# A layer kernel bound by TensorE: another table for the order of instructions on each engine

## The chip, the cores and the metric

One core of a Trainium2 chip runs the whole program. Its engines are TensorE (PE, with its weight loads PEld), VectorE (DVE), ScalarE (ACT), GpSimd (POOL) and SyncE (SP, which here only issues transfers). Times are microseconds on the device, the median over the executions shown. The trace comes from one further, profiled execution.

## The reference

One decoder layer on x of 512 tokens by 1024 channels, in float32. Two mixers read one input projection: native sparse attention with 8 heads of 64 (compressed blocks, the 8 best blocks, and a window, weighed by gates), and gated DeltaNet with 4 heads of 128. DeltaNet, cut to its core:

```python
qkv = jax.nn.silu(causal_dwconv(qkv, conv_w))        # a filter of 4 taps
T = lax.linalg.triangular_solve(eye + m, ...)        # inside each chunk
u, w = T @ (v * beta[..., None]), T @ (kb * jnp.exp(gcum)[..., None])
def step(state, xs):                                 # from chunk to chunk
    v_new = un - wn @ state
    o = (qn * jnp.exp(gn)[..., None]) @ state + an @ v_new
    state = state * jnp.exp(g_last)[..., None] + kn'.T @ v_new
```

The two results are merged with gates and projected, and x <- LN(alpha*x + mix). Then a gated MLP of width 2816 with a causal filter of width 3 follows, and a second LN.

## The kernel before

**Products.** A float32 product is made of fp32r matmuls. A weight block arrives as `raw` (SP's transfer, 128x1024), and `split_w` (L458) makes two halves of it: `wh` is the rounded part (L468 on ACT, L470 elsewhere) and `wl` what is left (L472). `product` (L477) then issues three matmuls for each k: L482 with wh, L484 with the activations' low part, L485 with wl. Small products and transposes run as fp32 with 128 columns or fewer: L657 transposes the DeltaNet tiles, L1073 the attention scores.

**Stages.** Up to about 320 us the program works through attention heads (`scores` and `attn`: L1040 and L1041 make scores, L1044 to L1057 the softmax, L1076 and L1077 the split of the transposed scores, L1087 and L1093 the sums over values) and DeltaNet heads (`gdn_mid`, `gdn_tri`, `gdn_inv`, `gdn_out`), mixed with each other and with the input projection. Then come the rest of the projection, the merge (L1119, L1197, L1199), the output projection and a LN, the FFN's up-projections with filter and gate (L1405 to L1414, some 480 to 700 us), and the down-projection with the last LN.

**The state recurrence.** `gdn_out` (L829) walks four chunks of a head. Each chunk is a chain: PE L838 multiplies by the state, DVE L840 makes r, PE L844 multiplies by z, ACT L846 copies it as vn, PE L854 makes the step, DVE L857 the new state, then the next chunk. L849 and L862 make the output beside it. `conv_silu` (L633) filters a head's input: ACT scales a tap (L640), POOL adds it (L641), ACT makes a tanh (L646), POOL multiplies (L650). In `gdn_inv`, L771 to L792 solve the triangular system; DVE's L788 makes ym, which PE's L791 multiplies.

**Transfers.** SP issues the loads of weights into three `raw` buffers, and the stores of the result (L1497). POOL issues sums of weight blocks in DRAM (L501 for the output projection's osum, L511 for the down-projection's wsum), some of which add to what an earlier one wrote and so wait for it.

**What sets the order.** Each engine runs its instructions strictly in its own order. `QUEUES` (from L133) is a table of numbers: for each engine the positions, in the order in which the code issues them, that are to run one after another. `queues` (L335) walks it and ties each instruction to the one ahead of it, for scheduling alone. Whatever else an instruction waits for (data, buffers) stays as it is.

Of the kernel before, what the change touches and what calls it, by code (L numbers as in the profile page):

```python
# [144 lines left out]
746 761 560-561 762-764 552 765-768 562 565-566 553 769 554 537-538 563 539 564 540 567 591-592 581-582 568-569 555  # L145
570 593-596 556 597 557 598 558 770-771 599-600 583 559 585-586 772 796-798 773 571-572 584 573 587 574-577 774
601-602 799-801 578 802 579 803 603 588 580 804 606 805 589 604 590 607 806-807 651 808-809 652 810 608 605 811-812
620-621 609-611 653 813-815 654 612 622-626 613-618 627-630 641-642 864-872 643-644 619 631 873 645-646 874 632-634
647-648 635 699 649-650 700 875 636-638 876 639-640 877-879 701 816 880 704 881 702-703 705 882-887 706 718-719
707-709 817-819 720 710 838-839 721-722 655-657 659 658 660-662 840 854 711 855 663-666 841 712-713 842 714 843 715  # L150
667-669 671-678 670 856 716 858 717 844-845 860 857 679-686 861 846 859 862 687-694 863 847-848 1053 695-698 747-750
936-938 1054 939-943 775-778 944-945 1055-1056 779 1057 946-948 780 949-951 781-782 1058-1059 849 952-954 783-784 977
955 978 785 956 979-981 786-787 1060 850 957 851 958 788-789 959 1072 790 982-983 1073 791-792 984-988 793 989-990
794-795 991-992 852 993-1008 853 1009 1074-1075 1061 1076 1062 820-821 824-825 1010-1012 822-823 826 1101 827-829 1029
1063 1102 830 832-833 831 1103-1108 1030 1013-1014 1031-1040 834 1015 835 1041-1045 836-837 1046-1050 888-890 1051
1064 1052 1065 891 1016-1018 1077-1100 1066 1019-1021 1067 1109-1111 1022 1068 1023-1024 1069-1070 892 896-897 893-895
898-899 1112 1203 1071 1205-1208 900-903 1209 1113 1204 1114-1115 1219 1116 1220 1117 1210 904 908-915 905-907
1211-1212 1221 1213 1223 1214 1118-1120 1224 916-923 1215-1217 1222 924-931 1121-1122 1218 932-935 1225-1226 1233-1234
1123 960 1227-1228 1124-1125 961 1126-1127 962-963 1128-1131 964-965 1132-1133 966 1141-1142 967-968 1134-1136
1143-1144 1235 969-970 1145-1147 971 1148-1150 1238 1151-1153 1236 972-973 1239 1179-1180 1237 974 1240 975 1241 1181  # L160
1252-1253 1154-1155 1182 1242 976 1243 1156 1183 1157-1158 1184-1185 1159 1186 1160-1162 1254 1187 1257 1163 1244-1245
1164 1188 1255-1256 1025 1137-1140 1259 1258 1246 1026 1189-1198 1283 1247 1199-1200 1273 1201 1274 1284 1202 1285
1027-1028 1165 1260 1166-1167 1248 1286 1261-1262 1307 1169-1170 1308-1311 1168 1171-1172 1275 1173 1249 1312 1250
1174 1251 1277-1278 1263 1287 1313-1315 1276 1175-1177 1279 1178 1316-1317 1403-1404 1318 1264 1319-1320 1405
1288-1289 1406 1280 1265-1267 1408 1268 1407 1281-1282 1269 1409 1270 1321-1323 1271 1324 1229 1325 1290 1272
1326-1327 1291 1328-1329 1230 1330 1410 1292 1422 1293 1423 1294 1231-1232 1424 1411-1413 1425-1426 1295-1298 1414
1299-1301 1427 1302-1304 1379 1428 1415 1380-1381 1416 1429-1432 1417-1419 1305 1382 1443 1420 1444 1331-1332 1421
1383 1306 1384-1385 1445 1386 1447-1448 1433 1387 1434 1388 1435 1389-1392 1436-1437 1333 1449 1446 1393 1453 1477
1454 1478 1394 1438 1450 1455-1456 1451 1439 1395 1458 1452 1440 1396-1397 1479 1459 1480 1441 1481 1442 1482 1334
1460-1462 1457 1463 1472-1473 1398 1483-1485 1399-1401 1486 1402 1487-1488 1474 1464 1501-1502 1465-1466 1475-1476  # L170
1467 1582 1489 1583 1490 1335 1503 1468 1517-1518 1339-1341 1504 1342 1336-1338 1505-1506 1491-1494 1343-1346
1519-1520 1469 1495 1521 1470 1347-1348 1522 1351-1358 1349 1471 1507-1508 1350 1509-1511 1496-1499 1512-1513
1359-1366 1523-1524 1544 1500 1545 1584-1585 1546 1367-1374 1525 1514 1547-1550 1610-1611 1515-1516 1586-1588
1375-1378 1551 1526 1612-1613 1527 1552-1554 1589 1614 1528 1615 1563-1564 1529-1530 1590 1616 1591-1592 1531-1532
1617-1618 1533 1555 1619 1593 1534 1594 1535 1556 1595 1620 1596 1536-1537 1597-1598 1538 1565 1599 1621-1622
1539-1540 1566-1567 1557-1558 1568-1569 1559 1600-1602 1541-1542 1570 1560 1571 1561 1623-1626 1543 1562 1603 1627
1604-1605 1572-1577 1628-1629 1634 1630 1635 1631 1636-1639 1632 1640-1641 1578 1606-1609 1579 1642-1643 1658 1644
1633 1645-1646 1580-1581 1647 1659-1660 1648 1661-1662 1649 1663-1667 1650-1651 1668-1670 1652-1654 1671 1682 1655
1672 1656-1657 1673-1675 1683-1685 1676-1680 1686-1687 1681 1694 1688-1692 1695 1693 1706-1707 1696 1708-1709 1718
1697-1698 1710-1711 1699-1700 1712-1714 1701 1715-1716 1702 1719 1703-1705 1720 1717 1721-1723 1730 1724-1728 1742  # L180
# [1389 lines left out]
```

## Time and profile before

| | us |
|---|---|
| median of 3 executions (lowest, highest) | 823.32 (821.67, 828.16) |
| the profiled execution | 826.54 |
| its span, first to last instruction | 824.8 |
| PE busy | 805.9 |
| DVE busy | 601.6 |
| ACT busy | 409.7 |
| POOL busy | 181.6 |

The mean granted clock of TensorE is 0.994 of full speed. An engine's busy time counts its instructions from start to end; a matmul that starts before the one ahead of it has ended doesn't count twice. In a timeline a row's time covers the instructions that are merged into it (x2, x3), and the brackets tell how long the engine stood idle ahead of it and what ended that.

### The profile page before, as it was taken

Reading aid. Unit: us, or ns where it says so; the run is one execution under the profiler, and the core shown is the slowest. Engines: PE = TensorE matmul, PEld = TensorE weight load, DVE = VectorE, ACT = ScalarE, POOL = GpSimd, SP = SyncE. Lnnn points to the kernel's source line nnn. Section 1 sums busy time; section 2 is a strip of 40 time slices with the busy share of each in tenths; the row PEclk is TensorE's granted clock in tenths of the full one; section 3 lists DMA queues with packets and bytes.
Section 4 is the critical chain, followed back from the end, with each engine's and each line's share of the span. In section 5 each row is a group of like instructions: output and inputs, shape, how many; then the busy total and the mean of one; then the engine's idle time right before and its main releaser. Section 6 shows DMA issues by size and latency. Waiting matters only on the chain.

```text
span 824.8 us, 11773 instructions
## 1 busy us (share of the span) xinstructions
PE 805.9 (98%) x4138; PEld 671.2 (81%) x4138; DVE 601.6 (73%) x1339; ACT 409.7 (50%) x912; POOL 181.6 (22%) x176
## 2 busy tenths in 40 slices
PE   9999999999899999999999999999999999999996
PEld 8788888787788888888787898888888888787774
DVE  5667689989858965565668955667566677687888
ACT  4453577774477764522344234344444444574641
POOL 0344834032283111052200111111111110100001
PEclk9999999999999999999999999999999999999998
DMA  8327180013577014344247482685238932475583
GB/s 280 106 79 281 63 268 27 26 52 125 111 183 182 27 52 103 128 140 135 83 182 250 130 165 86 235 182 163 89 112 240 222 103 90 140 212 171 185 257 132
DMA packets 43979, 119.58 MB, mean 145 GB/s; under 512 B 3472, under 2 KB 4624, under 8 KB 43664
## 3 DMA queue, kind: packets, MB, share of 16 engines
q1 hardware_dynamic: 32144, 87.37, 32.8%
q0 software_dynamic: 11776, 31.46, 16.6%
q8 instruction: 33, 0.54, 0.3%
q14 instruction: 26, 0.21, 0.1%
HBM read 116.72 MB, written 33.55 MB: 182 GB/s over the span
## 4 chain that ended last, share of the span: by engine, by line
PE 86%; DVE 6%; DMA 3%; ACT 2%; issue 1%; SPq 1%; POOL 0%; DVEq 0%; ACTq 0%
PE pu L484 10%; PE pu L482 10%; PE pu L485 10%; PE gps L482 9%; PE gps L484 9%; PE gps L485 8%; PE px L1450 5%; PE pz L1450 3%; PE pout L1087 2%; PE aps L1073 2%; PE pm L484 2%; PE pm L482 2%; PE pm L485 2%; PE pu L1450 2%; PE dps L657 1%; PE pw L1286 1%
## 5 line engine op out<-in xcount | busy, mean ns | idle before, releaser
L472 DVE TENSOR_TENSOR wl<-raw,wh 128x512 fp32r<-128x512 f32 x146 | 105.8, 728 | 74.0 <-PE pu L485 33.4
L468 ACT ACTIVATE wh<-raw 128x512 fp32r<-128x512 f32 x126 | 79.1, 629 | 140.7 <-PE pu L484 91.5
L485 PE MATMUL pu<-mh,wl 128*128 128x512 f32 (+1 forms) x384 | 130.9, 373 | 0.0
L484 PE MATMUL pu<-ml,wh 128*128 128x512 f32 (+1 forms) x384 | 130.9, 373 | 0.0
L482 PE MATMUL pu<-mh,wh 128*128 128x512 f32 (+1 forms) x384 | 130.4, 373 | 0.0
L482 PE MATMUL gps<-xh,wh 128*128 128x512 f32 x320 | 125.3, 402 | 2.4 <-ACT mt L1119 1.5
L484 PE MATMUL gps<-xl,wh 128*128 128x512 f32 x320 | 125.1, 400 | 0.0
L485 PE MATMUL gps<-xh,wl 128*128 128x512 f32 x320 | 123.2, 399 | 0.0
L485 PEld LDWEIGHTS pu<-mh,wl 128*128 128x128 f32 x384 | 71.5, 188 | 12.8
L482 PEld LDWEIGHTS pu<-mh,wh 128*128 128x128 f32 x384 | 71.3, 188 | 12.7
L484 PEld LDWEIGHTS pu<-ml,wh 128*128 128x128 f32 x384 | 71.2, 188 | 12.7 <-DVE ml L1266 0.2
L1414 POOL TENSOR_TENSOR fth<-fth,fa 128x512 f32<-128x512 f32 x22 | 31.3, 1429 | 211.7 <-DVE fth L1413 179.8
L1408 DVE SCALAR_TENSOR_TENSOR fa<-pu,fcw,fa 128x511 f32<-128x511 f32 (+1 forms) x88 | 64.5, 745 | 15.9 <-ACT fa L1405 15.4
L482 PEld LDWEIGHTS gps<-xh,wh 128*128 128x128 f32 x320 | 60.3, 189 | 13.9 <-issue 2.9
L485 PEld LDWEIGHTS gps<-xh,wl 128*128 128x128 f32 x320 | 60.2, 189 | 11.0 <-POOL wl L472 0.3
L484 PEld LDWEIGHTS gps<-xl,wh 128*128 128x128 f32 x320 | 60.4, 189 | 10.5
L1385 ACT ACTIVATE wh<-raw 128x512 fp32r<-128x512 f32 x67 | 40.2, 626 | 41.5 <-DMA raw<-wsum 12.0
L1386 DVE TENSOR_TENSOR wl<-raw,wh 128x512 fp32r<-128x512 f32 x67 | 44.8, 694 | 19.1 <-ACT wh L1385 18.5
L472 POOL TENSOR_TENSOR wl<-raw,wh 128x512 fp32r<-128x512 f32 x30 | 40.3, 1346 | 13.6 <-ACT wh L468 7.9
L523 POOL TENSOR_TENSOR rs<-rs,minus_half 128x1 f32<-128x1 f32 x8 | 7.3, 910 | 160.3 <-DVE rs L1244 108.2
L1046 ACT ACTIVATE sc<-sc,mn 128x384 f32<-128x384 f32 (+2 forms) x64 | 35.6, 558 | 9.9 <-DVE mn L1044 9.8
L1405 ACT ACTIVATE fa<-pu,fcw 128x512 f32<-128x512 f32 x44 | 29.6, 680 | 21.6 <-PE pu L485 18.3
(365 smaller groups left out, 1712.3 us busy)
## 6 DMA issues: line engine op xcount, KB each, us to landing
raw<-in_up SPq DMA_DIRECT2D x44, 512.0 KB, 3.8
raw<-in_wT SPq DMA_DIRECT2D x40, 512.0 KB, 3.6
wsum<-in_down POOLq DMA_DIRECT2D x6, 2816.0 KB, 21.8
raw<-wsum SPq DMA_DIRECT2D x20, 512.0 KB, 4.0
raw<-in_down SPq DMA_DIRECT2D x15, 512.0 KB, 4.1
osum<-in_wo POOLq DMA_DIRECT2D x6, 1024.0 KB, 9.9
wsum<-wsum POOLq DMA_DIRECT2D x2, 2816.0 KB, 14.2
raw<-in_wm SPq DMA_DIRECT2D x8, 512.0 KB, 3.5
```

The source lines that it names most:

```text
L468: A.activation(wh, r, AF.Copy)
L472: eng.tensor_tensor(wl, r, wh.bitcast(F32), op=OP.subtract)
L482: i = PE.matmul(ps, wh[k], mh_(k), start=(k == 0), stop=False)
L484: PE.matmul(ps, wh[k], ml_(k), start=False, stop=False)
L485: PE.matmul(ps, wl[k], mh_(k), start=False, stop=(k == n - 1))
L1046: A.activation(s[:, i, :n], s[:, i, :n], AF.Exp, scale=-1.0, bias=mn[:, 0, i:i + 1], accum_out=mn[:, 1, i:i + 1])
L1385: A.activation(hi, raw[:, i], AF.Copy)
L1386: V.tensor_tensor(lo, raw[:, i], hi.bitcast(F32), op=OP.subtract)
L1405: A.activation(acc, ps, AF.Copy, scale=w[:, 2:3])
L1408: V.scalar_tensor_tensor(acc[:, n:], ps[:, :S - n], w[:, i:i + 1], acc[:, n:], op0=OP.mult, op1=OP.add)
L1414: G.tensor_tensor(th, th, g[1], op=OP.mult)
L1450: m = PE.matmul(ps, a[x][:, j, ts], w[y], start=first and i == 0, stop=last and i == 2, skip_group_check=True)
```

## The change

Only the numbers in `QUEUES` differ, for all five queues, so the code below the table stands one line higher. The instructions, their operands and their buffers are the same. The order on PE is the same up to 126 us, on DVE up to 178, on ACT up to 202, on POOL up to 228 and on SP up to 799 us of the profiled execution. The table was made anew with two rules changed: a short GpSimd operation counts as handing its turn to the next one, and runs of fp32 work on TensorE are joined where that can be done. Two of its lines, as the diff shows them (the other rows are numbers of the same kind):

```diff
-37 140 62 26 41 45 54 48 55 42 36 49 51 47 52 64 66 65 67 46 68 57 69 58 50 53 56 59 61 108 104 63 109 75 60 76 80 92
+37 140 62 26 41 45 54 48 55 42 36 49 51 47 52 64 66 65 67 46 68 57 69 58 50 53 56 59 61 108 104 63 109 75 60 76 80 88
...
-173-178 168 179-180 172 182 166 170 181 183-184""",
+173-180 170 166 182 168 172 181 183-184""",
```

What that moves is seen in the engines' orders. In them gps is a product that is being summed up (2641 a projection, 2883 and 2971 two more), dps a DeltaNet product, aps and pout attention ones.

PE at about 202 us of the profiled execution, before:

```order
L482 MATMUL gps_2641<-xh_93,wh_2637 128x512
L657 MATMUL dps_2334<-ident_322,vraw_2290 128x128 x3
L484 MATMUL gps_2641<-xl_94,wh_2637 128x512
L1087 MATMUL pout_2700<-pth_345,vcat_108 128x512
L485 MATMUL gps_2641<-xh_93,wl_2639 128x512
L1087 MATMUL pout_2700<-ptl_346,vcat_108 128x512
L657 MATMUL dps_2334<-ident_322,vraw_2290 128x128
L482 MATMUL gps_2578<-xh_93,wh_2574 128x512
L484 MATMUL gps_2578<-xl_94,wh_2574 128x512
```

and now:

```order
L481 MATMUL gps_2641<-xh_93,wh_2637 128x512
L483 MATMUL gps_2641<-xl_94,wh_2637 128x512
L1086 MATMUL pout_2700<-pth_345,vcat_108 128x512
L484 MATMUL gps_2641<-xh_93,wl_2639 128x512
L1086 MATMUL pout_2700<-ptl_346,vcat_108 128x512
L656 MATMUL dps_2334<-ident_322,vraw_2290 128x128 x4
L481 MATMUL gps_2578<-xh_93,wh_2574 128x512
```

The four fp32 transposes of vraw stand together, where three and one stood before.

DVE at about 231.5 us, in the state recurrence of DeltaNet's head 2 (L857 makes the new state, L840 makes r), before:

```order
L840 SCALAR_TENSOR_TENSOR r_2473<-dps_2471,gk_1937,vb_2339 128x128
L875 SCALAR_TENSOR_TENSOR gs_2605<-gt_2603,gps_2578 128x512
L857 SCALAR_TENSOR_TENSOR state_2485<-state_2466,eg_341,dps_2483 128x128
L1048 RECIPROCAL mn_3131<-mn_3131 128x1
L1048 RECIPROCAL mn_3057<-mn_3057 128x1
L840 SCALAR_TENSOR_TENSOR r_2492<-dps_2490,gk_1937,vb_2339 128x128
L864 TENSOR_TENSOR ot_2459<-dps_2487,oi_2481 128x128
L1018 TENSOR_TENSOR pcl_2799<-aps_2793,pch_2798 128x512
```

and now:

```order
L839 SCALAR_TENSOR_TENSOR r_2473<-dps_2471,gk_1937,vb_2339 128x128
L865 COPY ot_2459<-dps_2468 128x128
L1047 RECIPROCAL mn_3057<-mn_3057 128x1
L1017 TENSOR_TENSOR pcl_2799<-aps_2793,pch_2798 128x512
L874 SCALAR_TENSOR_TENSOR gs_2605<-gt_2603,gps_2578 128x512
L1076 TENSOR_TENSOR ptl_346<-aps_3064,pth_345 128x2x2x128
L856 SCALAR_TENSOR_TENSOR state_2485<-state_2466,eg_341,dps_2483 128x128
L1098 TENSOR_TENSOR oT_2255<-pout_2700,ob_3029 64x512
L1047 RECIPROCAL mn_3131<-mn_3131 128x1
L863 TENSOR_TENSOR ot_2459<-dps_2487,oi_2481 128x128
L839 SCALAR_TENSOR_TENSOR r_2492<-dps_2490,gk_1937,vb_2339 128x128
```

Three whole-tile operations stand between the first r and the new state, where one stood, and another one ahead of the second r.

POOL at about 231.5 to 247 us, before:

```order
L501 DMA osum3_107<-osum2_106 512x512
L511 DMA wsum0_100<-in_down 1408x1x512
L1057 TENSOR_SCALAR sc_3056<-sc_3056,mn_3057,gsig_109 128x384
L472 TENSOR_TENSOR wl_2881<-raw_2873,wh_2879 128x512
L472 TENSOR_TENSOR wl_2965<-raw_2961,wh_2963 128x512
L641 TENSOR_TENSOR acc_2838<-acc_2838,tap_2842 128x509
L650 TENSOR_TENSOR th_2845<-th_2845,acc_2838 128x512
L501 DMA osum0_104<-in_wo 512x1x512
L1066 CAST vm_111<-vcb_344 32x128
```

and now:

```order
L1056 TENSOR_SCALAR sc_3056<-sc_3056,mn_3057,gsig_109 128x384
L500 DMA osum3_107<-osum2_106 512x512
L471 TENSOR_TENSOR wl_2881<-raw_2873,wh_2879 128x512
L640 TENSOR_TENSOR acc_2838<-acc_2838,tap_2842 128x509
L471 TENSOR_TENSOR wl_2965<-raw_2961,wh_2963 128x512
L649 TENSOR_TENSOR th_2845<-th_2845,acc_2838 128x512
L650 TENSOR_TENSOR kq_2802<-th_2845,acc_2838 128x4x128
```

Two issues and a CAST have gone from here to later places, and the tap-add has changed places with the weight split behind which it stood.

## Rows read from the trace of the kernel before

**Rows 1.** The page: busy time, share of the span and instructions of each engine; and the chain that ended last, by engine.

```profile
PE 805.9 (98%) x4138; PEld 671.2 (81%) x4138; DVE 601.6 (73%) x1339; ACT 409.7 (50%) x912; POOL 181.6 (22%) x176
...
PE 86%; DVE 6%; DMA 3%; ACT 2%; issue 1%; SPq 1%; POOL 0%; DVEq 0%; ACTq 0%
```

**Rows 2.** Busy time by stretch. Columns: the stretch, its length, then busy us (instructions) of PE, PEld, DVE, ACT and POOL, the granted clock, the DMA share and GB/s.

```profile
126.00:228.00 102.00, 96.57 (x610) 80.27 (x609) 91.21 (x282) 64.64 (x180) 30.65 (x33) 0.98 0.26 73
228.00:323.00 95.00, 95.00 (x580) 80.40 (x578) 71.32 (x239) 65.00 (x186) 33.36 (x35) 1.00 0.47 106
...
480.00:700.00 220.00, 220.00 (x1012) 183.58 (x1011) 144.76 (x236) 92.41 (x158) 30.89 (x22) 1.00 0.58 156
```

**Rows 3.** Who waited for whom, PE's two longest. Columns: the waiting instruction, what it waited for, us in total, times, the longest.

```profile
PE dps L791 <- DVE ym L788: 2.4, 1, 2.4
PE gps L482 <- ACT mt L1119: 1.5, 1, 1.5
```

**Rows 4.** The timeline from 211 to 218 us: POOL, then one row of DVE, then one of PE. Columns: start, us, engine, line, operation, out<-in.

```profile
212.47 1.16 POOL L470 CAST wh<-raw 128x512 fp32r<-128x512 f32 x1
213.03 1.82 POOL L741 TENSOR_TENSOR at<-at,cst 128x512 f32<-128x512 f32 x1
214.27 1.80 POOL L472 TENSOR_TENSOR wl<-raw,wh 128x512 fp32r<-128x512 f32 x1
...
212.48 4.15 DVE L472 TENSOR_TENSOR wl<-raw,wh 128x512 fp32r<-128x512 f32 x1
...
217.11 1.08 PE L791 MATMUL dps<-ym,x 128*128 128x64 f32 x8 [2.43 <-DVE ym L788]
```

**Rows 5.** Busy time of the four microseconds behind it, columns as in rows 2.

```profile
218.00:222.00 4.00, 4.00 (x13) 2.95 (x12) 2.55 (x12) 0.88 (x4) 0.00 (x0) 0.57 0.53 97
```

**Rows 6.** The timeline of PE around 202 us and, in its last two rows, at 306.77 us.

```profile
201.87 0.39 PE L482 MATMUL gps<-xh,wh 128*128 128x512 f32 x1
...
203.70 0.39 PE L484 MATMUL gps<-xl,wh 128*128 128x512 f32 x1
...
204.16 0.40 PE L482 MATMUL gps<-xh,wh 128*128 128x512 f32 x1
...
208.96 0.39 PE L482 MATMUL gps<-xh,wh 128*128 128x512 f32 x1
...
306.77 0.38 PE L844 MATMUL dps<-vb,z 128*128 128x128 f32 x2
306.99 0.49 PE L1073 MATMUL aps<-ident,sc 128*128 128x128 f32 x3
```

**Rows 7.** The timeline of DeltaNet's head 2, 231 to 243 us: PE, then DVE, then ACT.

```profile
233.18 0.38 PE L854 MATMUL dps<-vn,kd 128*128 128x128 f32 x2
...
234.08 0.41 PE L838 MATMUL dps<-state,kq 128*128 128x128 f32 x2
...
239.85 0.39 PE L844 MATMUL dps<-r,z 128*128 128x128 f32 x2
...
242.03 0.39 PE L862 MATMUL dps<-vn,at 128*128 128x128 f32 x2
...
233.60 0.35 DVE L857 SCALAR_TENSOR_TENSOR state<-state,eg,dps 128x128 f32<-128x128 f32 x1 [1.01 <-PE dps L854]
...
234.99 0.68 DVE L1018 TENSOR_TENSOR pcl<-aps,pch 128x512 fp32r<-128x512 f32 x1
...
239.88 0.63 ACT L646 ACTIVATE th<-acc 128x512 f32<-128x512 f32 x1 [0.59 <-POOL acc L641]
240.41 0.26 ACT L846 ACTIVATE vn<-dps 128x128 f32<-128x128 f32 x1
```

**Rows 8.** The timeline of POOL, 232 to 269 us.

```profile
232.41 1.75 POOL L511 DMA_DIRECT2D wsum<-in_down  x1
...
236.97 1.30 POOL L472 TENSOR_TENSOR wl<-raw,wh 128x512 fp32r<-128x512 f32 x1 [0.76 <-ACT wh L468]
238.56 1.28 POOL L641 TENSOR_TENSOR acc<-acc,tap 128x509 f32<-128x509 f32 x1 [0.29 <-ACT tap L640]
240.58 1.30 POOL L650 TENSOR_TENSOR th<-th,acc 128x512 f32<-128x512 f32 x1 [0.74 <-ACT th L646]
241.83 1.22 POOL L501 DMA_DIRECT2D osum<-in_wo  x1
...
268.16 0.61 POOL L470 CAST wh<-raw 128x512 fp32r<-128x512 f32 x1 [3.97 <-issue]
```

**Rows 9.** Transfers of weight blocks: the view of issues (KB each, median us from issue to landing) for 232 to 254 us and for 262 to 300 us, then the issue at 263.87 and the first reader of its block in the timeline.

```profile
raw<-in_wT SPq DMA_DIRECT2D x3, 512.0 KB, 7.2
...
raw<-in_wT SPq DMA_DIRECT2D x3, 512.0 KB, 3.5
...
263.87 0.33 SPq L461 DMA_DIRECT2D raw<-in_wT  x1
...
288.89 0.63 ACT L468 ACTIVATE wh<-raw 128x512 fp32r<-128x512 f32 x1
```

**Rows 10.** The FFN's beginning: POOL's first L1414 and the ACT instruction that waits for it, in the timeline, and the transfer that POOL had issued before, in the view of issues.

```profile
494.30 1.75 POOL L1414 TENSOR_TENSOR fth<-fth,fa 128x512 f32<-128x512 f32 x1 [16.94 <-DVE fth L1413]
...
509.06 0.67 ACT L1405 ACTIVATE fa<-pu,fcw 128x512 f32<-128x512 f32 x1
...
wsum<-in_down POOLq DMA_DIRECT2D x1, 2816.0 KB, 20.6
```

More of the change, by code (lines that the diff above doesn't have):

```diff
@@ new lines @@
+1308 1170 1309-1312 1275 1171-1174 1277-1278 1313-1314 1287 1315-1317 1175-1176 1276 1279-1280 1177-1178 1251 1263
+1403-1404 1264 1318-1319 1265-1266 1281 1405-1406 1282 1407 1267-1268 1408 1269 1409 1270 1288 1320-1322 1289-1290
+1323 1271-1272 1229 1324-1329 1410 1330 1230 1422 1291-1293 1423 1411-1412 1424-1425 1413 1426 1231 1294-1295
+1427-1428 1232 1296-1297 1414 1298-1300 1379 1301 1380 1302-1303 1381 1304-1305 1415-1417 1429-1432 1418 1382
+1443-1445 1331 1419 1306 1383-1384 1447 1420 1448 1421 1433 1385 1434 1386-1387 1477 1388-1389 1478 1390-1391 1435
@@ new lines @@
+1811-1812 1819-1820 1793 1821 1813 1822-1823 1826 1794 1824 1827 1825 1795 1828 1796 1829-1830 1797-1801 1831-1837
+1850-1851 1838 1852 1839 1853-1855 1840 1856-1859 1841 1860-1862 1842 1863 1843-1844 1864 1845 1874 1846 1875 1847
+1876 1865 1848 1877 1849 1866 1878-1880 1867 1881-1882 1868 1886 1883 1887-1888 1884 1889-1892 1885 1893-1894 1898
+1895-1896 1899 1869 1900 1870 1897 1901-1907 1871-1872 1908-1910 1873 1911-1915 1922 1916-1917 1923 1918 1924
+1919-1920 1925-1929 1921 1930-1932 1946-1947 1933 1948-1951 1934 1952 1935 1958-1960 1953 1936 1961-1966 1954
@@ new lines @@
+2087 2115 2098 2102 2078 2116 2079-2080 2118 2084 2105 2119 2103 2085 2123 2120 2086 2088-2089 2121 2104 2106-2107
+2124-2125 2129-2131 2122 2108-2110 2135 2141 2111-2112 2138 2136 2113 2126 2139 2127 2142-2143 2128 2147 2137
+2132-2133 2148 2140 2144 2134 2145-2146 2150 2149 2151-2153 2162 2154 2156-2157 2155 2163 2158-2161 2164 2168-2170
+2174-2176 2180-2182 2189-2190 2165-2167 2171-2173 2186-2187 2177-2179 2188 2183 2192-2194 2198 2184 2191 2185 2199
+2195 2200 2204 2196-2197 2205-2206 2201-2202 2210-2213 2203 2207-2209 2218-2220 2224-2225 2221-2222 2226 2223
@@ new lines @@
+2506 2497 2507-2508 2472 2509 2498-2499 2473 2457 2510 2474 2500 2511-2514 2501 2475 2502 2515-2517 2476 2503-2504
+2477 2518 2505 2478 2519-2521 2479-2481 2530-2533 2522 2534 2523-2524 2535-2539 2525 2540-2541 2526 2542-2543 2527
+2544-2545 2554-2555 2528-2529 2556-2557 2546 2558-2559 2547-2550 2560-2563 2551 2564-2565 2552-2553 2566-2570
+2578-2581 2571 2582-2586 2572 2587-2591 2573 2592-2593 2602-2603 2574-2575 2604 2576 2605 2577 2606 2594 2607
+2595-2596 2608-2613 2597-2599 2614-2615 2626-2627 2600 2616 2628-2632 2601 2633 2617-2619 2634-2635 2620-2621
@@ new lines @@
+2636-2637 2622 2638 2623 2639 2650 2624 2651 2640 2625 2652-2653 2641-2642 2654-2655 2643-2644 2656-2659 2645
+2660-2661 2646-2647 2662-2663 2674 2648 2664-2666 2649 2667-2670 2675-2676 2671 2677-2679 2672-2673 2680-2685 2698
+2686 2699-2702 2687 2703-2705 2688 2706-2711 2689-2690 2712 2691 2722-2723 2713 2724 2714 2692-2693 2715 2694 2716
+2725-2728 2695-2696 2717 2697 2729-2733 2718-2719 2734 2720 2735 2746 2736 2747-2749 2737-2739 2721 2750-2752 2740
+2753-2754 2741 2755-2756 2742 2757-2758 2743 2759-2763 2770-2777 2744 2778-2780 2745 2781 2764-2766 2794 2782
@@ new lines @@
+2946 2912 2947 2913 2948 2931 2949-2950 2932-2933 2962-2963 2934-2935 2951-2952 2964 2953 2936 2965-2966 2954
+2967-2970 2955 2971-2972 2937 2956-2958 2973 2959 2986 2974 2960 2975 2961 2987-2990 2976-2977 2991-2993 2978-2980
+2994-2995 2981 2996 2982 2997-2998 2983 2999-3001 2984 3002 3010 3003 2985 3004 3011 3005-3006 3012 3007 3013-3014
+3008-3009 3015-3018 3034 3019-3020 3035 3021-3022 3036 3023 3037-3044 3024 3045 3025 3046 3026 3058 3047-3048 3027
+3059-3060 3028-3029 3061 3030 3049 3031-3032 3062-3063 3050 3033 3051-3052 3064-3065 3053 3066-3068 3054-3055
@@ new lines @@
+3069-3071 3082 3056-3057 3072 3083-3092 3073-3074 3093 3075-3076 3106-3107 3077-3079 3108 3094-3097 3109-3112 3080
+3113 3098 3081 3114-3115 3099 3116-3117 3100-3103 3130 3104-3105 3118 3131-3135 3119 3136-3140 3120-3121 3141-3143
+3154 3122-3123 3155 3124 3156 3125 3144 3157 3126-3128 3158 3129 3159-3160 3145 3161-3164 3146 3165-3167 3147 3178
+3168 3148 3169-3170 3179-3181 3171 3149 3172 3182 3150-3153 3183-3185 3173 3186-3191 3174-3177 3202 3192-3199
+3203-3204 3200 3205-3210 3201 3211-3212 3226 3213-3219 3227-3232 3220-3225 3233-3236 3250 3237-3238 3251-3252
@@ new lines @@
+3239-3240 3253-3262 3241-3242 3263-3264 3274-3275 3243 3276-3277 3244 3265 3245 3278-3279 3246 3280 3247-3248 3281
+3266 3282 3249 3267 3283-3287 3268-3269 3288 3270-3271 3298 3289 3272 3290 3299-3303 3273 3304-3305 3291 3306 3292
+3307 3293-3295 3308 3296-3297 3309-3313 3322 3314 3323-3327 3315 3328 3316 3329-3334 3317 3335-3338 3318-3319
+3339-3340 3320 3346 3341 3321 3342-3344 3347 3345 3348-3353 3370 3354-3358 3371-3373 3359-3360 3374 3361-3362
+3375-3380 3363 3381 3364-3366 3394-3395 3382 3396 3383 3397 3384 3398-3399 3367-3369 3400-3402 3385 3403-3404 3386
@@ L321 @@
[L321 to L324 removed]
+302 240 232-233 273-274 234 241 275 235 305 276 242 286 303 287-288 306 243 289 252 244 304 245-246 312 311 314 313
```

285 lines of the change are left out of this document (120 added, 165 removed), and 3 rows, old and new, of the table QUEUES.

## The prediction

> **What bounds the kernel now.** I read the page's busy times and chain first: PE is busy for 805.9 us of the span, 98%, and 86% of the chain that ended last is PE [rows 1]. So a term counts only if it changes what PE waits for, or how long PE's own instructions take. Then I cut the span where the two orders part company. PE's own queue is the same up to 126 us, and between 126 and 228 us only a few instructions are exchanged. From 228 to 323 us (two DeltaNet heads mixed with attention) all five compute queues are reordered. From 480 to 700 us (the FFN's up-projections) PE's matmuls are exchanged by the hundred, but between two products that are both ready. The table of busy time by stretch shows what each has to give [rows 2]: 126 to 228 us has 102.00 - 96.57 = 5.43 us of PE idle time; 228 to 323 us has none (95.00 of 95.00); 480 to 700 us has none (220.00 of 220.00). The stretch that changes most has nothing idle to win back.
>
> The list of who waited for whom names the idle time: 2.4 us for DVE's ym (L788) and 1.5 us for ACT's mt (L1119) are the two longest [rows 3]. The timeline shows how the first one comes about [rows 4]: DVE's weight split L472 begins at 212.48, beside a Pool CAST that begins at 212.47, and takes 4.15 us, until Pool's L470, L741 and L472 have all gone by; ym stands behind it on DVE, and PE's L791 begins at 217.11 after 2.43 us of idleness. From 218 to 222 us the granted clock is 0.57 [rows 5], between full speed (2.4 GHz) and half (1.2 GHz): a loss of 0.43 x 4.00 = 1.7 us. This place is worth 2.4 + 1.7 = 4.1 us.
>
> **The change, part by part.** No instruction is added, removed or resized, so the terms are waits and changeovers alone.
>
> *The big waits.* The Pool run L470, L741, L472 and its DVE partners stand in the same order in both programs, and so do the instructions on the chain that ends in the wait for mt. I cost the two waits as unchanged: 0. The bounds are -4.1 us (see the first rival) and 0.
>
> *fp32 runs joined.* Counted over the whole order, PE's fp32 instructions stand in 169 runs before and in 135 after. A changeover's price: from the L482 at 201.87 to the L484 at 203.70 there are six 512-column fp32r matmuls and four fp32 transposes in two runs, 1.83 us [rows 6]. The pure fp32r stretch from 204.16 to 208.96 has 21 steps of 0.2286 us; two fp32 matmuls take 0.22 us from 306.77 to 306.99 [rows 6], 0.11 each. 6 x 0.2286 + 4 x 0.11 = 1.81, so two runs cost 0.02 us, 0.01 each. 34 runs fewer give -0.3 us; bounds 0 and -0.7 (twice the price, for the rounding).
>
> *The state recurrence of head 2, 231 to 243 us.* Each step is PE L844, ACT L846, PE L854, DVE L857, PE L838, DVE L840, and PE again. Before, other matmuls just cover it: L854 begins at 233.18, L857 begins at 233.60 and takes 0.35, and L838 begins at 234.08 [rows 7], 0.13 after L857's end; there is no slack to spare. The change moves three whole-tile DVE operations (L1018, L875, L1077; L1018's row is 0.68) ahead of this L857, and one (L1099) ahead of L840. It also moves two 512-column matmuls (0.2286 each) ahead of L854, which is work done early, not lost: L854 then begins at 233.18 + 0.46 = 233.64, and its product is there for L857 at 234.06, after the same 0.42 as before. One more matmul covers the next link: L838 could begin at 233.64 + 0.90 + 0.23 = 234.77. Walked by hand with the durations of rows, DVE is through with the first L840 and two short operations at about 232.55, and three whole-tile operations at 0.6 from start to start (0.68, less some 0.08 by which such rows overlap) put L857 at 234.35; with its 0.35 and the 0.13 to PE that makes 234.83 for L838, not quite 0.1 late. L1099 and two short operations put L840 some 0.3 late, of which the covering matmuls take a third: 0.2. At the fourth step, L844 to L862 took 242.03 - 239.85 = 2.18 us before [rows 7], with much between them; after, only L849 and four transposes stand there, about 0.8, and ACT's L646 (0.63) still precedes L846 (0.26) [rows 7] and still waits for Pool's L641: 0.1 to 0.6. Sum: +0.8 us; bounds 0.3 (each operation at its earliest) and 1.3.
>
> *Pool at the same place.* The tap-add L641 (1.28) now precedes the split L472 of wl_2965 (1.30) [rows 8]. PE reads that split, in the new order, one place behind L862, at about 241.3 by the walk. Pool then needs ACT's tap by 241.3 - 1.3 - 1.3 = 238.7; before it came in time for 238.56. That is 0.14 us of room: +0.1, in the 0.8 above.
>
> *Pool's DMA issues.* The issue of wsum0 (1.75 us) leaves 232.41 and one of osum0 (1.22 us) leaves 241.83 [rows 8]. The wsum0 issue and one for osum3 now stand ahead of the CAST at 268.16, which had 3.97 us of idleness ahead of it [rows 8]: 1.75 + 1.2 fit, cost 0. The transfers they start run beside the raw weight loads; a raw load amid such transfers landed after 7.2 us [rows 9], and the one issued at 263.87 is first read at 288.89 [rows 9], so the cover is 17 us: 0. Without that cover it would be the 3.7 us by which 7.2 exceeds an undisturbed load's 3.5 [rows 9]. In the FFN the issue wsum2<-wsum1 is moved ahead of three L1414 products, and it waits for the transfer before it: that was issued until about 477.4 (494.30 less 16.94) and lands 20.6 us after its start [rows 10], about 496.2. With an issue like the 1.22 us one [rows 8] the first L1414 starts at about 497.4 in place of 494.30, 3.1 us late. Who waits for it is ACT's fa at 509.06 [rows 10]: 509.06 - 497.4 - 1.75 leaves 9.9 us, so 0.
>
> *The rest.* The FFN's exchanges: 0, since PE had no idle time there and both products' splits are made in the same order up to a few places. SP's last stores: two stores that were issued late are issued earlier and two early ones later, four still follow the last normalisation's release, and the two that end the kernel are the same: 0. Between 245 and 323 us I did not walk every link; the like of head 2 recurs once (head 3 at 306 us), so I put +0.5 there, bounds -0.3 (an fp32 switch or two) and +4.1 (one more stall of the size and clock loss of the one at 214 us).
>
> Sum against the profiled execution: 826.54 - 0.3 + 0.8 + 0.5 = 827.5. That execution lies 3.2 us above the median of the runs, 823.32, so the forecast is 824.3, rounded to **824**: no change that can be told. About 1% (8.2 us, the three runs shown span 6.5) is what a measurement here can tell from none.
>
> **The rivals.** *Faster: the race at 212.48 falls the other way.* DVE's split began 0.01 us after Pool's CAST [rows 4]. The instructions ahead of it on PE and DVE, from 178 and 202 us on, are exchanged a little; if DVE now begins some hundredths earlier, its split takes about 0.7, ym is out in time, and wait and clock loss go together: 824 - 4.1 = 820. For it: the gap is tiny. Against: that order is itself unchanged, and both sides hang on the same PE products. To pass 1% every other wait within the 5.43 us of 126 to 228 us would have to go as well.
>
> *Slower: Pool's queue keeps PE waiting.* The new order L641, L472, L650 makes the weight split wait for an activation. Place: PE's first L485 with wl_2965, and the like in head 3. It decides once ACT's tap ends after 238.7; each us later is a us of PE. Two L472-sized operations late is 2.6 us, past the 2.4 us wait after which the clock fell [rows 4, 5], so 2.6 + 1.7 = 4.3 a head; one head gives 824 + 4.3 = 828, both 832.6. For it: tap now stands behind more on ACT and DVE. Against: Pool loses two DMA issues there.
>
> The trace bears on how long DVE can be held in such a run: one split stood through three Pool operations, 4.15 us [rows 4] where another whole-tile operation takes 0.68 [rows 7], some 3.5 us too long. The Trainium skill (SBUF — State Buffer, "Who interferes with whom") says that the port DVE and GpSimd share is an exclusive lock which whoever issues first holds for its whole instruction. By it DVE should have had its turn after the CAST of 1.16 us, and the stall would have been some 2 us shorter. The row disagrees: DVE waited through a run. By the row a DVE operation caught beside the new run L641, L472, L650 could lose 1.28 + 1.30 + 1.30 = 3.9 us, by the rule 1.3 at most.
>
> *The order does nothing:* the exchanges lie in ready work only. Then only the joins count, 823; I hold it with the forecast.
>
> **Chances.** Forecast (821.5 to 827.5): 0.66. First rival 0.19, of which 0.05 beyond 1%. Second rival 0.15, of which 0.08 beyond 1%. So faster 0.05, slower 0.08, the same 0.87. The range 818.5 to 829.5 takes in the first rival's 820, the second's 828 and the bounds of the sum; about 0.17 is left outside.
>
> **What would show it.** Right: PE idle from 228 to 323 us of 0.5 to 2 us, in pieces under 0.6 at L844, L862 and L485; still 2.4 us ahead of L791 with the clock down behind it; nothing new after 323. Wrong: a DVE split of 0.7 us at 212 us (first rival), a PE wait of over 2 us with a low clock in the 228 to 323 us stretch (second), or a wait for L1414 in the FFN.

## The result, and the profile after

The changed kernel takes 820.71 us (818.83 to 825.38, 20 executions), the kernel before 826.15 us (821.46 to 828.58, 20 executions beside it). The ratio of the means is 0.9949, with a 95% interval of 0.9931 to 0.9967: faster by about 4.2 us, half a per cent. The forecast said that no change could be told. The time lies in the range, but the direction was missed. Two executions among the runs below, one of 2846.76 us (e12) and one of 3382.2 us (e15), are left out of all that follows.

The profiled execution of the changed kernel took 824.98 us, 1.6 us less than that of before. So the first thing to see is that its profile holds less than half of the gain. Code lines stand one lower than before (L471 is the old L472).

The page after, the two lines that answer to [rows 1]:

```profile
PE 804.0 (98%) x4138; PEld 672.5 (82%) x4138; DVE 602.7 (73%) x1339; ACT 409.0 (50%) x912; POOL 179.5 (22%) x176
...
PE 81%; DVE 10%; DMA 5%; ACT 2%; issue 2%; SPq 0%; POOL 0%; DVEq 0%; ACTq 0%; POOLq 0%
```

Busy time by stretch after, as [rows 2], and PE's two longest waits, as [rows 3]:

```profile
126.00:228.00 102.00, 96.54 (x603) 80.97 (x602) 90.57 (x281) 63.73 (x177) 29.71 (x32) 0.97 0.26 70
228.00:323.00 95.00, 95.00 (x582) 81.48 (x582) 71.74 (x238) 65.94 (x188) 33.31 (x35) 1.00 0.49 112
...
480.00:700.00 220.00, 219.85 (x1010) 183.20 (x1009) 143.44 (x232) 90.93 (x157) 29.87 (x22) 1.00 0.58 156
```

```profile
PE dps L790 <- DVE ym L787: 2.5, 1, 2.5
PE gps L481 <- ACT mt L1118: 1.5, 1, 1.5
```

All of this looks as before: the reordered stretch has no idle PE, the two waits stand. In the timeline the split is held up as in [rows 4], and the clock is at half (0.50, 1.2 GHz) from 218 to 222 us, lower than in [rows 5]:

```profile
212.41 1.16 POOL L469 CAST wh<-raw 128x512 fp32r<-128x512 f32 x1
212.98 1.82 POOL L740 TENSOR_TENSOR at<-at,cst 128x512 f32<-128x512 f32 x1
214.21 1.81 POOL L471 TENSOR_TENSOR wl<-raw,wh 128x512 fp32r<-128x512 f32 x1
...
212.41 4.17 DVE L471 TENSOR_TENSOR wl<-raw,wh 128x512 fp32r<-128x512 f32 x1
...
217.06 1.30 PE L790 MATMUL dps<-ym,x 128*128 128x64 f32 x5 [2.46 <-DVE ym L787]
```

```profile
214.00:218.00 4.00, 1.54 (x11) 1.33 (x9) 3.96 (x4) 1.23 (x3) 2.02 (x2) 0.75 0.97 163
218.00:222.00 4.00, 4.00 (x13) 3.42 (x13) 2.19 (x10) 0.88 (x4) 0.00 (x0) 0.50 0.52 97
222.00:226.00 4.00, 4.00 (x49) 3.11 (x48) 2.05 (x9) 2.00 (x8) 0.00 (x0) 0.90 0.00 0
```

One place where the two profiles part is a stretch that the prediction's table did not have, the down-projection. Before, then after:

```profile
700.00:745.00 45.00, 44.53 (x195) 36.11 (x194) 32.65 (x55) 27.93 (x46) 5.45 (x4) 1.00 0.59 181
745.00:810.00 65.00, 64.71 (x278) 51.09 (x277) 54.44 (x85) 32.66 (x53) 1.54 (x2) 1.00 0.64 199
```

```profile
700.00:745.00 45.00, 44.62 (x196) 36.10 (x195) 34.59 (x58) 26.51 (x46) 6.45 (x4) 1.00 0.55 168
745.00:810.00 65.00, 64.94 (x286) 53.15 (x286) 55.14 (x86) 34.03 (x55) 1.54 (x2) 1.00 0.67 202
```

PE's busy time hides it (64.71 against 64.94); the count shows it: 286 matmuls run in the same 65 us where 278 did, and the weight loads are busy for 53.15 us instead of 51.09. The waits of 745 to 811 us say why. Before, the weight loads wait for DVE's splits; after, the longest such wait is one of 0.5 us for ACT:

```profile
PEld px L1450 <- DVE wl L1386: 1.8, 5, 0.7
...
PEld px L1450 <- DVE w L1386: 0.8, 2, 0.4
```

```profile
PEld px L1449 <- ACT wh L1384: 0.5, 1, 0.5
```

The other place is the stretch from 228 to 323 us, where PE is busy throughout in both. The time between the same two matmuls, a product and a transpose, shows it; before, then after:

```profile
232.04 0.39 PE L482 MATMUL gps<-xh,wh 128*128 128x512 f32 x1
...
293.61 0.38 PE L1073 MATMUL aps<-ident,sc 128*128 128x128 f32 x2
```

```profile
232.97 0.39 PE L481 MATMUL gps<-xh,wh 128*128 128x512 f32 x1
...
293.63 0.27 PE L1072 MATMUL aps<-ident,sc 128*128 128x128 f32 x1
```

That is 61.57 us before and 60.66 after. In all ten profiles with the new order there, of this kernel and those below, it is 60.59 to 60.69 us, in the ten with the old one 61.45 to 61.57: a gain of 0.9 us which no idle time shows.

**Two groups.** The times do not scatter round one value; they fall into two groups, for which I take cuts at 824.5 and 823 us. Of all 130 executions of the kernel before, beside this and the runs below, 24 lie below 824.5 us (median 822.3) and 106 above (median 827.1). Of 41 of the changed kernel, 22 lie below 823 (median 820.6) and 19 above (median 825.1). Each group has moved by 1.7 to 2.0 us, and the lower one is more often met. The two had to be told apart.

### The profile page after: what moved, and what is told of

Read it like the earlier page. It is cut to its first block, busy times and chain, and to the rows that moved or that the text cites. A ratio compares the mean times of both kernels' runs of the same rounds, so it can differ in the third digit from the quotient of the medians.

```text
span 823.2 us, 11781 instructions
## 1 busy us (share of the span) xinstructions
PE 804.0 (98%) x4138; PEld 672.5 (82%) x4138; DVE 602.7 (73%) x1339; ACT 409.0 (50%) x912; POOL 179.5 (22%) x176
## 4 chain that ended last, share of the span: by engine, by line
PE 81%; DVE 10%; DMA 5%; ACT 2%; issue 2%; SPq 0%; POOL 0%; DVEq 0%; ACTq 0%; POOLq 0%
PE pu L483 9%; PE pu L481 9%; PE pu L484 9%; PE gps L481 9%; PE gps L483 8%; PE gps L484 8%; PE pout L1086 2%; PE pz L1449 2%; PE px L1449 2%; PE aps L1072 2%; PE pm L481 2%; PE pm L483 2%; PE pm L484 2%; DVE wl L1385 2%; PE dps L656 1%
## 5 line engine op out<-in xcount | busy, mean ns | idle before, releaser
L471 DVE TENSOR_TENSOR wl<-raw,wh 128x512 fp32r<-128x512 f32 x146 | 106.4, 735 | 73.3 <-ACT wh L467 40.9
L481 PEld LDWEIGHTS pu<-mh,wh 128*128 128x128 f32 x384 | 71.0, 188 | 12.6
L483 PEld LDWEIGHTS pu<-ml,wh 128*128 128x128 f32 x384 | 71.0, 188 | 12.6
L1413 POOL TENSOR_TENSOR fth<-fth,fa 128x512 f32<-128x512 f32 x22 | 31.2, 1427 | 196.9 <-DVE fth L1412 193.9
L1385 DVE TENSOR_TENSOR wl<-raw,wh 128x512 fp32r<-128x512 f32 x67 | 44.3, 691 | 14.5 <-ACT wh L1384 14.2
L471 POOL TENSOR_TENSOR wl<-raw,wh 128x512 fp32r<-128x512 f32 x30 | 40.0, 1336 | 13.5 <-ACT wh L467 7.1
```

Of the source, the lines that this page charges most:

```text
L471: eng.tensor_tensor(wl, r, wh.bitcast(F32), op=OP.subtract)
L481: i = PE.matmul(ps, wh[k], mh_(k), start=(k == 0), stop=False)
L483: PE.matmul(ps, wh[k], ml_(k), start=False, stop=False)
L1385: V.tensor_tensor(lo, raw[:, i], hi.bitcast(F32), op=OP.subtract)
L1413: G.tensor_tensor(th, th, g[1], op=OP.mult)
```

## The experiments

Two theories at the outset. "Tail": the gain is made in the down-projection. "Clock": the new order makes the clock's fall behind the wait for ym rarer. The kernels of the runs are called e1 to e18.

**The change in three pieces (e1, e2, e3).** The two tables have places where every queue has run the same instructions in both; there they can be joined.

```diff
 # e1; the cuts (some 335 and 707 us): PE 1683 3413, DVE 718 1122, Activation 453 701, Pool 114 164, SP 58 137
-QUEUES["PE"] = before
+QUEUES["PE"] = after[:1683] + before[1683:]                 # the other queues likewise
 # e2
+QUEUES["PE"] = before[:1683] + after[1683:3413] + before[3413:]
 # e3
+QUEUES["PE"] = before[:3413] + after[3413:]
```

> The new order on all five queues up to about 335 us of the kernel before (the attention and DeltaNet stages), the old order from there on. Theory 'tail' (the gain is made in the down-projection): ratio 1.000, within 1 us. Theory 'clock' (the new order makes the clock's fall behind the wait for ym rarer): the mean over many executions falls by 2 to 3 us, ratio 0.997, with more executions at a granted clock of 0.997 or 0.998 instead of 0.994 to 0.996. The forecast's walk of the state recurrence would make it 1 us slower.

> The new order between about 335 and 707 us only (rest of the projection, merge, output projection, up-projections). Both theories: within 0.5 us of the kernel before, ratio 1.000; the one wait of 0.3 us that the changed kernel's profile shows at 504 us may show, +0.4 us.

> The new order from about 707 us on only (the last up-projections, the down-projection, the last LN). Theory 'tail': 2.1 us faster, ratio 0.9975, PE's waits for DVE's weight splits L1386 from 700 to 811 us mostly gone. Theory 'clock': no difference, ratio 1.000.

Ratios: e1 0.998 (0.9955 to 1.0006), e2 1.0011 (0.9991 to 1.0032), e3 0.9998 (0.9975 to 1.0021). By these alone nothing is told, and the 0.9975 that "tail" asked of e3 was missed: an interval of half a per cent is made of the two groups. The profiles told more. That of e1 took 820.68 us, and is one of the lower group. Its timeline at the place of [rows 4], and its clock:

```profile
212.10 1.16 POOL L469 CAST wh<-raw 128x512 fp32r<-128x512 f32 x1
213.20 1.29 POOL L740 TENSOR_TENSOR at<-at,cst 128x512 f32<-128x512 f32 x1
214.45 1.28 POOL L471 TENSOR_TENSOR wl<-raw,wh 128x512 fp32r<-128x512 f32 x1
...
212.07 0.69 DVE L471 TENSOR_TENSOR wl<-raw,wh 128x512 fp32r<-128x512 f32 x1
213.12 0.42 DVE L787 TENSOR_TENSOR ym<-dps,cst 128x256 f32<-128x256 f32 x1 [0.36 <-PE dps L785]
...
214.10 1.00 PE L790 MATMUL dps<-ym,x 128*128 128x64 f32 x8
```

```profile
214.00:218.00 4.00, 4.00 (x35) 3.37 (x35) 3.56 (x16) 2.03 (x7) 1.73 (x2) 1.00 1.04 181
218.00:222.00 4.00, 4.00 (x59) 3.17 (x53) 2.47 (x10) 3.00 (x11) 0.00 (x0) 1.00 0.50 88
```

Here DVE's split begins 0.03 us ahead of the CAST. It takes 0.69 us instead of 4.17. The CAST's own row has 1.16 us in either case, but the next POOL operation begins 1.10 us behind its start, where it was 0.57. ym is out at 213.5, PE does not wait, and the clock stays at 1.00 (2.4 GHz). In the profiles of e2 (827.43 us) and e3 (828.24 us) the split is 0.01 and 0.02 us behind the CAST and takes 4.15 and 4.13. So the groups look like the two ways in which a race falls, that of the split and the CAST, from one execution to the next of the same kernel. Of the twenty profiles the seven with a held split have the wait for ym and a lower clock behind it, the thirteen others neither; the same PE work, from 212.1 to 223.3 us of the profile before, takes 11.1 to 12.6 us in the seven and 6.8 to 6.9 in the thirteen.

**The race taken away (e4).** The edit that the expectation names is not what the kernel carried: ym and the split kept their places, and the RECIPROCAL L1008 was moved up by one.

```diff
 # e4, DVE in the order of the kernel, about 208 us
 L1007 TENSOR_REDUCE csm_2787<-cs_2778 128x16
+L1008 RECIPROCAL csm_2787<-csm_2787 128x16
 L770 TENSOR_TENSOR tmp_2189<-lx_2170,xs_2187 128x4x12
-L1008 RECIPROCAL csm_2787<-csm_2787 128x16
```

> The kernel before with one exchange on DVE alone: ym (L788) stands ahead of the weight split L472 that took 4.15 us at 212.48. If the wait for ym costs what the forecast's first rival says (2.4 us of wait and 1.7 us of clock), 4.1 us faster, ratio 0.995, and all executions at one granted clock; if the split is late for PE instead, the wait only moves to L485 some matmuls later and the gain is under 1 us.

822.42 us, eleven executions all between 821.44 and 823.40; ratio 0.9957 (0.9935 to 0.9979), where 0.995 was expected. The triangular solve ends later, and POOL's CAST with it: 212.82 where it was 212.47. The split begins at 212.63 where it was 212.48, but all of this execution already stands 0.17 us later at 203 us, so the CAST is some 0.2 us later and the split is not. It is now first by 0.19 us in the profile. One group is left, the lower one, with the clock at 1.00. That this place makes the groups is shown. (The edit that was meant, ym ahead of the split, was not tried.)

**The changed kernel again, and three kernels without the race (e5 to e8).** The last three carry the exchange of e4, not the one in the words of the expectation: e6 in the changed kernel, e7 with e3's piece, e8 with e1's.

> The changed kernel again, beside the kernel before on this chip. Theory 'two forms': its executions fall into two groups some 4.2 us apart, about 820.5 and 824.8, as the split on DVE gets ahead of GpSimd's CAST or not; half or more of them fall into the lower group, of the kernel before about three in ten. Theory 'tail alone': one group, 2 us below the kernel before's.

> The changed kernel with ym ahead of the weight split on DVE. Theory 'two forms': one group only, spread under 2.5 us, median 820.5 (822.4 of the same exchange in the kernel before, less 1.9 for the tail), granted clock 0.997 or 0.998. Rival 'the early part gains by itself': below 820.

> The kernel before with ym ahead of the split (822.4 in the other run) and the new order from 707 us on. One group; theory 'tail': 1.7 to 2.1 us less than 822.4, about 820.5. Rival 'the tail gives nothing (its single profile differed by chance)': 822.4.

> The kernel before with ym ahead of the split and the new order up to 335 us. One group; theory 'the early part matters through the race alone': 822.1 to 822.4 (the joined fp32 runs may give 0.3). The forecast's walk of the state recurrence: 823.2 to 823.7.

e5: 825.1 us, ratio 0.9977 (0.9957 to 0.9996); two groups as expected, but only 2 of 11 in the lower one, beside 3 of 17 of the kernel before. The share was missed. e6: 820.92 us (818.74 to 821.43), one group near the 820.5 expected, its spread a little over 2.5 us. e7: 821.91 us, between its two predictions. e8: 821.26 us, below both of its own. But e4's 822.42 came from another chip, so the pieces had to be measured beside each other:

**The pieces on one chip (e9, e10, e11).** e9 is e4 again; e10 is e8 and e11 is e7.

> The kernel of the run e4 again, described by what its edit does: on DVE the RECIPROCAL of csm (L1008, the compressed scores, some 208 us) stands one place earlier, between two steps of the triangular solve; the split and ym keep their places. The solve's last step, and with it GpSimd's z, DMA issue and CAST, come 0.3 us later, the split on DVE 0.15 us. Theory 'race': the split now begins before the CAST in every execution, so one group, about 822, as in e4 (822.4). It is the base for the next two runs on this chip.

> That exchange with the new order up to about 335 us. One group. Theory 'each part gives a little': 0.7 us below e9, as the profiles show 0.7 us less of stretched or idle matmuls from 215 to 335 us (5.2 to 5.7 against 6.0 to 6.4). Rival 'only the race': equal to e9.

> That exchange with the new order from about 707 us on. One group. Theory 'each part gives a little': 1.0 to 1.5 us below e9 (stretched or idle matmul time from 700 us on is 1.5 to 3.0 us in five profiles of the new tail and 3.0 to 5.5 us in five of the old one). Rival 'only the race': equal to e9.

e9 822.85 us (822.39 to 824.80), e10 822.49 (820.87 to 823.30), e11 820.67 (819.96 to 822.43). By these medians of five the tail is worth 2.2 us (1.0 to 1.5 was expected) and the early part 0.4 (0.7 was expected), within the scatter. Busy time from 745 to 810 us, e9 and then e11:

```profile
745.00:810.00 65.00, 64.62 (x279) 51.42 (x278) 54.91 (x86) 31.86 (x52) 1.54 (x2) 1.00 0.64 198
```

```profile
745.00:810.00 65.00, 64.91 (x283) 52.52 (x282) 56.35 (x89) 32.29 (x52) 2.38 (x3) 1.00 0.62 197
```

This holds over all profiles: nine with the old order there have 273 to 283 matmuls in these 65 us (278.4 in the mean), eleven with the new one 282 to 286 (283.5). Five matmuls at the 0.2286 us of the prediction are 1.2 us. The time from the matmul at 745.6 us of the profile before to PE's last one says the same: 70.6 us in the mean of the nine, 69.3 in that of the eleven, so 1.3 us. PE and its weight loads wait there for DVE for 1.0 to 5.2 us in the nine and for 0.2 to 1.1 in the eleven.

The early part's 0.4 is a sum. Where two orders are joined at 335 us (e1, e2, e8 and e10), PE takes 9.1 us from 329.2 to 337.8 us of the profile before; in the sixteen others it takes 8.6. This joint hides 0.5 of the 0.9 us that the order from 232 to 294 us gains.

**Another order on GpSimd (e12).**

```diff
 # e12, POOL in the order of the changed kernel, about 212 us
 L772 TENSOR_TENSOR z_2220<-xs_2187,cst_320 128x512
+L469 CAST wh_2875<-raw_2873 128x512
 L500 DMA osum2_106<-in_wo 512x1x512
-L469 CAST wh_2875<-raw_2873 128x512
```

> The changed kernel with one exchange on GpSimd: the CAST L469 stands ahead of the DMA issue L500 (at 211.75 us) instead of behind it, so the CAST is over about when DVE's split begins and the issue stands beside the split. Theory 'race': the split takes under 1 us in every execution, no wait for ym, one group about 820.5 on this chip's scale (1.5 to 2 us below e9). Rival 'a run of GpSimd operations holds DVE whatever its first one is': the split still takes 3 us or more, 825.

A miss: two groups again (ratio 0.9955, 0.9933 to 0.9977), five executions from 819.53 to 821.02 and six from 823.73 to 827.59. Its profile is of the lower group:

```profile
212.46 0.60 POOL L469 CAST wh<-raw 128x512 fp32r<-128x512 f32 x1
213.01 1.20 POOL L500 DMA_DIRECT2D osum<-in_wo  x1
213.69 1.82 POOL L740 TENSOR_TENSOR at<-at,cst 128x512 f32<-128x512 f32 x1
...
213.09 0.69 DVE L471 TENSOR_TENSOR wl<-raw,wh 128x512 fp32r<-128x512 f32 x1
```

The CAST now takes its 0.60 us and is over as the split begins. The two still meet within 0.03 us (213.06 and 213.09), so a race is possible there as well. What holds the split in the other group no profile here shows.

**Does the join move the race? (e13 to e16)**

```diff
 # e14, PE in the order of the kernel before, about 202 us (e15 does the reverse in the changed kernel)
-L657 MATMUL dps_2334<-ident_322,vraw_2290 128x128 x3
 L484 MATMUL gps_2641<-xl_94,wh_2637 128x512
...
-L657 MATMUL dps_2334<-ident_322,vraw_2290 128x128
+L657 MATMUL dps_2334<-ident_322,vraw_2290 128x128 x4
```

> The changed kernel on another chip. Theory 'the new order moves the race': half or more of its executions in the faster form (about 820.5, the other 824.8), and more of them than of the kernel before. Rival 'the chip alone decides': the same share as the kernel before beside it, and a ratio of 0.9975.

> The kernel before with one edit on PE: the three transposes of vraw at 202 us stand with the fourth. Theory 'the join moves the race': PE is 0.01 to 0.02 us earlier at the product that kl waits for, so the faster form (822.5) comes up more often than in the kernel before. Rival: the same share. Either way the two forms themselves stay where they are, 822.5 and 827.

> The changed kernel with that run parted again, three and one. Theory 'the join moves the race': a smaller share of the faster form than e13. Rival: the same share as e13. The forms at 820.5 and 824.8.

> The changed kernel with the RECIPROCAL of csm one place earlier on DVE, the edit of e9. One group; 2.0 to 2.5 us below e9's 822.85, 820.5, and faster than both kernels: ratio to the kernel before 0.992 to 0.993.

e13: 823.9 us, ratio 0.996 (0.9939 to 0.9981); 4 of 10 in the lower group, less than the half expected. e14: ratio 0.9966 (0.9948 to 0.9985); 6 of 12 below 824.5, where the kernel before had 2 of 25 beside it. e15: ratio 0.9972 (0.9959 to 0.9985); none of 8 in the lower group. In the profile of e14 the split (211.91) is 0.04 us ahead of the CAST, in e15's both begin at 211.88 and the split takes 4.16. The join does make PE earlier, by 0.02 us: the work from 201.87 to 203.39 us of the profile before takes 1.49 to 1.50 us in the ten profiles with it and 1.52 to 1.53 in those without. That is of the size of the gaps between the split and the CAST, and e14 met the lower group more often than the kernel before beside it. But e15's none of 8 beside e13's 4 of 10 can be chance, so that the joined run moves the race is likely, and not shown. What it does elsewhere stays open too: the changed kernel met its lower group in 16 of 20, 2 of 11 and 4 of 10 executions on three occasions. e16: 820.67 us, ratio 0.992 (0.9901 to 0.9939). It beats both kernels, as expected: only the lower group is left, and its split is 0.23 us ahead:

```profile
212.43 1.15 POOL L469 CAST wh<-raw 128x512 fp32r<-128x512 f32 x1
...
212.20 0.80 DVE L471 TENSOR_TENSOR wl<-raw,wh 128x512 fp32r<-128x512 f32 x1
```

**The tail in two (e17, e18).** Both with the exchange of e4; the cut at 745 us is PE 3574, DVE 1179, Activation 746, Pool 166, SP 152.

```diff
 # e17
+QUEUES["PE"] = before[:3413] + after[3413:3574] + before[3574:]
 # e18
+QUEUES["PE"] = before[:3574] + after[3574:]                 # the other queues likewise
```

> The edit of e9 and the new order from about 707 to 745 us only (the last up-projections, the first products of the down-projection). Theory 'the waits for weight splits at 710 and 722 us go': 0.5 to 1.0 us below the 822.85 of e9, ratio about 0.994 to 0.9945. Rival 'all of the gain is later': as e9, ratio 0.9955.

> The edit of e9 and the new order from about 745 us on only (the rest of the down-projection, the last stores). Theory 'the waits at 760 to 778 and 808 to 811 us go': 1.0 to 1.5 us below e9, ratio about 0.9935. Rival 'all of the gain is earlier': as e9, ratio 0.9955.

e17: 823.76 us, ratio 0.9955, as e9; e18: 821.63 us, ratio 0.9931, as e11. e17 pays for its second joint, 11.5 us from 745.6 to 755.9 us of the profile before where all others take 10.2 to 10.7. But from 707 to 745 us the new order gains nothing in any case (39.0 us in the mean of eleven profiles, 39.1 in that of the nine others). So the tail's gain is made from 745 us on, in the down-projection.

## Why the prediction was wrong

By terms the forecast came to +1.0 us (-0.3, +0.8, +0.5, and 0 for the waits and the rest). What the first measurement and the profiles show is about -2.0 for the share of the race, -0.9 from 232 to 294 us, +0.5 in the FFN and -1.3 in the down-projection: -3.7 us, where -4.2 was measured. That 820.71 lies in the range is in part luck, since the kernel before it came to 826.15 us in 20 executions and not to the 823.32 of three.

**A step that failed: "The rest".** It costed the exchanges behind 480 us at nothing, "since PE had no idle time there". That was read from 480 to 700 us [rows 2]. The stretch from 745 us on was in no row of the argument, although its order changes on PE, DVE and ACT up to the end, and there PE did wait for weight splits. Measured: -2.2 us by the medians (e11 against e9), -1.3 by the profiles, from 745 us on (e18). SP's stores, which move there too, have no part in it: from PE's last matmul to the end it is 8.3 or 8.4 us in all twenty profiles.

**A second: "the two waits as unchanged: 0".** Half right. The wait for mt is the same. The wait for ym is there in some executions and not in others, of the same kernel; a term of the sum can't be 0 or -4.1 when it is a share of 4.5 to 4.8 (the distance of the groups). The first rival named the place and the cause rightly (the gap of 0.01 us), and its 4.1 us is near the distance; 0.19 was too little for it. The price is more where the clock stays down for longer, as in the profile after. But the rival took the fall of the race as one answer for a kernel. The share could not be weighed from one profile; the three times shown, 821.67 to 828.16 us, were a sign of it. At the first measurement the share rose from 7 of 20 to 16 of 20, 0.45 x 4.5 = 2.0 us of the 4.2. On other chips it gave less, and the ratio was 0.996 and 0.9977 there.

**"fp32 runs joined", -0.3.** The one join that was tried apart gives 0.02 us (e14), twice the price; 34 of them would be the bound of -0.7. What was overlooked is that the sides of the race stand only 0.00 to 0.04 us apart in the profiles, so that so small a step may decide it.

**A third: the state recurrence, +0.8, and the links up to 323 us, +0.5.** Wrong in sign: nothing was lost. From 232.04 to 246.29 us of the profile before, the ten profiles with the new order take 13.9 us and the others 14.2, and up to 293.61 us the gain grows to 0.9. Some ten fp32 runs fewer stand there, 0.2 us at 0.02 each; what gives the rest was not tried apart. After, the links of [rows 7] read:

```profile
234.57 0.38 PE L853 MATMUL dps<-vn,kd 128*128 128x128 f32 x2
235.49 0.38 PE L861 MATMUL dps<-vn,at 128*128 128x128 f32 x2
235.71 0.39 PE L837 MATMUL dps<-state,kq 128*128 128x128 f32 x2
...
232.48 0.35 DVE L839 SCALAR_TENSOR_TENSOR r<-dps,gk,vb 128x128 f32<-128x128 f32 x1
233.01 0.67 DVE L1017 TENSOR_TENSOR pcl<-aps,pch 128x512 fp32r<-128x512 f32 x1
...
234.19 0.68 DVE L1076 TENSOR_TENSOR ptl<-aps,pth 128x512 fp32r<-128x512 f32 x1
234.99 0.35 DVE L856 SCALAR_TENSOR_TENSOR state<-state,eg,dps 128x128 f32<-128x128 f32 x1
```

The three whole-tile operations are over at 234.87, and the new state begins at 234.99, 0.42 behind L853, as before; L837 follows L853 by 1.14, what the matmuls between them take. This profile stands 0.93 us later than that of before (232.97 against 232.04). The walk had DVE through with the first r and two short operations at 232.55; the next operation, L1017, begins at 233.01, which is 232.08 on the walk's scale. So DVE had 0.47 us more than the walk gave it, and no link was late.

**GpSimd's transfers and the FFN.** Right as to the transfers. The two issues stand from 264.15 to 267.16, and 0.91 us of idleness are left ahead of the CAST; the issue for wsum2 waits until 496.22 (forecast 496.2), and no one waits for the L1413 behind it:

```profile
264.15 1.24 POOL L500 DMA_DIRECT2D osum<-in_wo  x1
264.89 2.27 POOL L510 DMA_DIRECT2D wsum<-in_down  x1
268.07 0.61 POOL L469 CAST wh<-raw 128x512 fp32r<-128x512 f32 x1 [0.91 <-issue]
...
496.22 0.90 POOL L510 DMA_DIRECT2D wsum<-wsum  x1 [18.90 <-DMA wsum<-in_down]
502.30 1.29 POOL L1413 TENSOR_TENSOR fth<-fth,fa 128x512 f32<-128x512 f32 x1 [5.18 <-DVE fth L1412]
...
502.70 1.44 DVE L471 TENSOR_TENSOR wl<-raw,wh 128x512 fp32r<-128x512 f32 x1 [0.55 <-ACT wh L467]
...
504.19 0.50 PE L484 MATMUL pu<-mh,wl 128*128 128x512 f32 x1 [0.15 <-DVE wl L471]
```

But the FFN's exchanges were not free. In the last two rows a weight split of DVE, begun 0.40 us behind that L1413, takes 1.44 us instead of some 0.69, and PE waits for DVE's splits. Up to 505.6 us of the profile before, from 481.5 on, the eight profiles with the new order take 24.5 us and the twelve with the old one 24.1; up to 707 us it is 0.5 us more. The forecast had asked who waits for the product, and not who is held beside it.

**The second rival** (GpSimd's queue keeps PE waiting) did not come: PE is busy 95.00 of 95.00 us from 228 to 323.

## What to carry to other kernels

Give every stretch in which an order changes its own row, the last one too, and take the time between the same two instructions in both profiles: the busy share of PE hid here what that showed. Kernels pieced together from two orders can pay at the joint, so look there before the pieces are compared. Where two engines begin within a few hundredths of a microsecond of each other and one can hold the other, be ready for two groups of executions and ask for the share, not for a sign; a single profile shows one of them. Take such a race away (here by one small instruction moved by one place) before measuring anything smaller than the distance of the groups.

## What the runs showed of the hardware

DVE's weight split has both inputs in SBUF. Where it begins together with a GpSimd CAST or up to 0.03 us behind it, it stands through three GpSimd operations in a row, 4.13 to 4.17 us in seven profiles; it takes 0.69 to 0.80 us in the twelve where it begins 0.03 us or more ahead. At 502 us, behind a single GpSimd operation, it takes 1.44 us and ends 0.55 us after it. The Trainium skill (SBUF — State Buffer, "Who interferes with whom") lets the one that comes first hold the port for its instruction; the runs agree that the first is served first, and at 212 us they show a longer hold.

The granted clock fell to half (1.2 GHz) behind the 2.4 us wait in all seven profiles that have the wait, for differing lengths: the mean over 218 to 222 us is 0.57 in the profile before, 0.50 in that after and 0.50 to 0.70 in all seven. It stayed at 1.00 there in the thirteen without the wait. Neither of the two orders settled which of the two an execution would be.
